# Two running totals as split single-pass matmuls, one slab part ordered behind a small one, and three products moved between VectorE and GpSimd

## The chip, the cores and the metric

The kernel runs on one core of one Trainium2 chip. The metric is the device time in microseconds (us) of one launch that computes two whole layers. Three runs of the kernel before gave 1693.34, 1693.60 and 1693.99 us; their median is 1693.6 us.

Engine names follow the profile: PE is the matmul engine (TensorE) and PEld its weight loads, DVE is VectorE, ACT is ScalarE, POOL is GpSimd, SP is the engine that issues the large loads.

## What is computed

A decoder trunk of two equal layers over 512 tokens of width 1024, all in float32. In each layer four token mixers share one input projection; the change touches three of them.

```python
def ssd_chunked(x, dt, a, bmat, cmat):            # Mamba-2 branch
    cs = jnp.cumsum(dtf * a.reshape(ng, r), axis=2)
    ...
def gla_chunked(q, k, v, log_a):                  # gated linear attention
    b = jnp.cumsum(log_a.reshape(bsz, nc, CHUNK, nh, dk), axis=2)
    b_last = b[:, :, -1]
    q_dec = qf * jnp.exp(b)
    k_inv = kf * jnp.exp(-b)
    k_end = kf * jnp.exp(b_last[:, :, None] - b)
    ...
def forgetting_attention(q, k, v, f_logit, q_gain, k_gain):
    qf = rms_norm(q, q_gain) * (dh ** -0.5)
    kf = rms_norm(k, k_gain)
    s = jnp.einsum('bhqd,bkhd->bhqk', q_blk, kf) + c_blk[..., :, None] - ck[..., None, :]
    ...
```

After the mixers come the gated merge, an output projection, and a feed-forward block of hidden width 2816.

## The kernel before, in words

**Weights.** All weights stream from HBM in slabs of 8 blocks of 128x128 (tile `wr`). `convert()` turns a slab into two parts: ACT casts a high part `wh` in the type float32r (`split`, line 208), and DVE subtracts it from the original to make a low part `wl` (line 209). `block()` hands out the blocks in order and asks for slabs two ahead of the one in use. Every projection is then three float32r matmuls for one block (`mm3`: high by high, high by low, low by high), 512 columns wide. `mm2` is the form with two matmuls, where one operand is exact in the high part alone and the other is a pair (high, low). A matmul whose operands are plain float32 goes through the same line 194, and the trace shows it as two records of TensorE.

**Order.** Each branch is a generator: `ssd()`, `gla()`, `ret()`, `fox()`, one after the other. `drain()` runs a branch, and at each `yield` it pulls some microseconds of filler from a list: projections of later branches, gate projections and up projections (`ups`, which ends in DVE line 1201). So the small matmuls of a branch stand between long runs of 512-column filler matmuls, and the chain of vector work between two yields has the filler as its cover. The framework plans the order of each engine's instructions ahead of the run, by its own timeline; each engine then runs its queue in that order. `order(a, b)` puts instruction `a` behind instruction `b` in the plan.

**The places of the change**, with the line numbers of the kernel before:

- In `ssd()`, line 707: the running total of `dta` (128 tokens by 32 columns) is one plain float32 matmul against `Uf`, a triangle of ones. `dts`, the split pair of the same `dta`, is already there for two other totals (`dflat`).
- In `gla()`, lines 863 to 866: `la` holds the logarithms of the gate in two tiles of 128x512; line 865 makes them on DVE. Line 873: four plain float32 matmuls for each `j` (0 and 1) form the running total in chunks of 64 with `ubd`, a block triangle of ones that float32r holds exactly. `la` is the stationary operand there. Lines 874 to 887 then form the decayed queries and keys; line 887 is the product for `k_end`, on POOL for both `j`. Line 915 transposes its results on PE.
- In `fox()`, line 1051 scales the query gain by 0.125, and line 1066 is the product of each of `q0`, `q1`, `k0`, `k1` (128x512) with its gain and its inverse norm, on DVE. `newton` (lines 373 to 375) refines the inverse norm just before. `stack()` (lines 1074 to 1084) splits the results for the scores.
- In `fox()`, `value()`: three calls for each head `hd`, with `runs` starting at (0, 0), (0, 2) and (2, 2). Each transposes probabilities, splits them (lines 208 and 209, widths 384, 512 and 384) and multiplies the values.

Of the kernel before, what the change touches and what calls it, by code (L numbers as in the profile page):

```python
# [10 lines left out]
F32 = mybir.dt.float32  # L11
# [3 lines left out]
ALU = mybir.AluOpType  # L15
# [3 lines left out]
P = 128  # L19
# [109 lines left out]
def trunk(ctx: ExitStack, tc: tile.TileContext, keys, qkeys, xin, pos, wst, wsq, par, ext, cst, out):  # L129
    nc = tc.nc  # L130
    V, A, G, T = nc.vector, nc.scalar, nc.gpsimd, nc.tensor
# [61 lines left out]
    def mm(o, l, r, start, stop):  # L193
        T.matmul(o, lhsT=l, rhs=r, start=start, stop=stop, skip_group_check=True)  # L194
# [7 lines left out]
    def mm2(o, l, r, start, stop):  # L202
        pairs = [(a, r) for a in l] if isinstance(l, tuple) else [(l, b) for b in r]
        for i, (a, b) in enumerate(pairs):
            mm(o, a, b, start and i == 0, stop and i == 1)

    def split(src, hi, lo):
        seen["copy"] = A.copy(out=hi, in_=src)  # L208
        V.tensor_tensor(out=lo, in0=src, in1=hi.bitcast(F32), op=ALU.subtract)  # L209
        return hi, lo  # L210

    def split_tile(t):
        return split(t, TT(F32R), TT(F32R))
# [4 lines left out]
    seen = {"set": None, "last": None}  # L218

    def order(a, b):  # L220
        tc.add_manual_dep(a.ins, b.ins.name, mybir.DependencyInfo(mybir.DependencyClass.NoSync, mybir.DependencyReason.DATA), reason="table")
# [31 lines left out]
    def convert():  # L253
        n = len(ready)
        if n < SLABS:
            far = n % (BLOCKS // SLAB) in TOKEN
            hi, lo = (piece("wh", 16), piece("wl", 48)) if far else (piece("wh"), piece("wl"))
            for h in halves(n):
                split(raw[n][:, h], hi[:, h], lo[:, h])
            ready.append((hi, lo))  # L260
            raw[n] = None

# [33 lines left out]
    o, w = PAR_OFF["ln1"]  # L296
# [47 lines left out]
    lst, bones, ubd, uo = (R(n) for n in ("lst", "bones", "ubd", "uo"))  # L344
    sel8 = R("sel8").rearrange("p (g r) -> p r g", g=2)
    sel4, selc = R("sel4"), R("selc")
    U, ones = uo[:, :P], uo[:, P:2 * P]
    Uf = U.bitcast(F32)
# [96 lines left out]
    def layer(l, n1, scope):  # L445
# [5 lines left out]
        def PR(n):  # L451
            o, w = PAR_OFF[n]
            return pr[:, l, o:o + w]
# [153 lines left out]
        dta = SM([P, NB, 8], "dta", 1)  # L607
# [6 lines left out]
        ps = MX()  # L614
# [62 lines left out]
        def ssd():  # L677
            Bt, Ct = xs[4], xs[5]
            pw = MX()
            dflat = tuple(t.rearrange("p c h -> p (c h)") for t in dts)  # L680
# [15 lines left out]
            for ps in pcb:  # L696
                t = TT()
# [3 lines left out]
            ps = MX()  # L701
# [2 lines left out]
            btok = TT()  # L704
            A.copy(out=btok, in_=ps)
            ps = MX()
            mm(ps[:32, :P], dta.rearrange("p c h -> p (c h)"), Uf, True, True)
            rows = stacked_rows(ps, 32, "blk8")
            heads = stacked_rows(ps, 32, "blkc", "blkc")
            ch, cl = (sp.tile([32, P], F32R, tag=n, name=nm(n), bufs=1) for n in ("csh", "csl"))  # L710
# [10 lines left out]
            for c in range(NB):  # L721
                ps = MX()
                for i in range(4):
                    T.transpose(ps[:, i * P:(i + 1) * P], xs[i][:, c * P:(c + 1) * P], ident)  # L724
                t = TT()
# [17 lines left out]
            for c in range(NB - 1):  # L743
                ps = parts[c]
                t = hp[c // 2][:, (c % 2) * 256:(c % 2 + 1) * 256]
# [8 lines left out]
            for r in range(4):  # L754
                ps = MX()
                mm(ps[:, P:], sel[:, r * P:(r + 1) * P], rows[:, P:], True, True)
                t = TT()
# [64 lines left out]
            for g in range(2):  # L822
                sq = []
                for ii in range(2):
                    t = TT()
# [6 lines left out]
            for g in range(2):  # L832
                ps = MX()
# [3 lines left out]
            for g in range(2):  # L837
                r = rstd_of(pn[g], 256)
                for ii in range(2):
                    i = 2 * g + ii  # L840
# [4 lines left out]
        gq, gk = [None] * 2, [None] * 2  # L845
# [3 lines left out]
        def gla():  # L849
            la, pl = [], []  # L850
            for half in range(2):
                ps = MX()
                pv = ps.rearrange("p (c n) -> p c n", c=2)
                for b in range(2):
                    tb = 2 * half + b
                    mm(pv[:, b], glrT[:, tb * P:(tb + 1) * P], w2, True, True)
                pl.append(ps)
                t = TT()
# [4 lines left out]
            for h_, t in enumerate(la):  # L863
                act(out=t, in_=t, func=AF.Ln, bias=one)
                V.scalar_tensor_tensor(out=t, in0=pl[h_], scalar=0.0, in1=t, op0=ALU.min, op1=ALU.subtract)
                la[h_] = t
            yield 2
            qd, ki, ke, dcs = [], [], [], []
            for j in range(2):
                ps = MX()  # L870
                for tb in range(NB):
                    o = (tb % 2) * 256 + j * P
                    mm(ps[:, tb * P:(tb + 1) * P], la[tb // 2][:, o:o + P], ubd.bitcast(F32), True, True)
                e = TT()
                act(out=e, in_=ps, func=AF.Exp, scale=1.0 / 16)
                V.tensor_tensor(out=gq[j], in0=gq[j], in1=e, op=ALU.mult)
                en = TT()
                act(out=en, in_=ps, func=AF.Exp, scale=-1.0 / 16)
                V.tensor_tensor(out=en, in0=gk[j], in1=en, op=ALU.mult)
                bl = SM([P, 8], "bl", 2)  # L880
                p8 = ps.rearrange("p (n t) -> p n t", n=8)
                V.tensor_copy(out=bl, in_=p8[:, :, 63])
                dc = SM([P, 8], "dc", 2)
                act(out=dc, in_=bl, func=AF.Exp, scale=1.0 / 16)
                V.tensor_tensor(out=e.rearrange("p (n t) -> p n t", n=8), in0=bl.unsqueeze(2).broadcast_to([P, 8, 64]), in1=p8, op=ALU.subtract)
                act(out=e, in_=e, func=AF.Exp, scale=1.0 / 16)
                G.tensor_tensor(out=e, in0=gk[j], in1=e, op=ALU.mult)  # L887
                qd.append(gq[j])
                ki.append(en)
                ke.append(e)  # L890
                dcs.append(dc)
# [11 lines left out]
            for half, ps in enumerate(pa):  # L903
                t = TT()
                (A.copy if half else V.tensor_copy)(out=t, in_=ps)
                for par_ in range(2):
                    u = t[64 * par_:64 * par_ + 64]
# [4 lines left out]
            for j in range(2):  # L912
                ps = MX()
                for tb in range(NB):
                    T.transpose(ps[:, tb * P:(tb + 1) * P], ke[j][:, tb * P:(tb + 1) * P], ident)  # L915
                t = TT()
# [4 lines left out]
            for tb in range(NB):  # L921
                for j in reversed(range(2)):
                    for par_ in range(2 if tb < NB - 1 else 1):
                        rs = slice(64 * par_, 64 * par_ + 64)
                        pv = pk[par_].rearrange("p (c j n) -> p c j n", c=NB, j=2)
                        for half in range(2):
                            hd = 2 * j + half
# [18 lines left out]
            for j in range(2):  # L946
                for tb in range(NB):
                    for par_ in range(2):
                        rs = slice(64 * par_, 64 * par_ + 64)
                        for half in range(2):  # L950
                            hd = 2 * j + half
# [93 lines left out]
        def fox():  # L1045
# [2 lines left out]
            fox_squares()  # L1048
            yield
            g8 = SM([P, 1], "g8", 1)  # L1050
            V.tensor_scalar(out=g8, in0=PR("fqn"), scalar1=0.125, scalar2=None, op0=ALU.mult)
            qk = fq + fk
            pn = []
            for q in fsq:
                ps = MX()
# [3 lines left out]
            for ps in pn:  # L1059
                u = TT()  # L1060
                act(out=u, in_=ps, func=AF.Ln, scale=1.0 / 64, bias=eps)
                rs_.append(u)
            for i, u in enumerate(rs_):
                act(out=u, in_=u, func=AF.Exp, scale=-0.5)
                newton(u, pn[i], 64)
                V.scalar_tensor_tensor(out=qk[i], in0=qk[i], scalar=g8 if i < 2 else PR("fkn"), in1=u, op0=ALU.mult, op1=ALU.mult)
            yield 2

            stk = {}
# [36 lines left out]
            def value(hd, runs, zs, po):  # L1106
                ps, W = MX(), 0
                at = []
                for kb, q0 in runs:
                    at.append(W)  # L1110
                    for qb in range(q0, 2 * (q0 // 2) + 2):
                        T.transpose(ps[:, W:W + P], zs[qb][:, kb * P:(kb + 1) * P], ident)  # L1112
                        W += P
                hi, lo = TT(F32R), TT(F32R)
                split(ps[:, :W], hi[:, :W], lo[:, :W])
                for (kb, q0), o in zip(runs, at):
                    q1 = 2 * (q0 // 2) + 2
                    n = (q1 - q0) * P
                    cols = slice(q0 * P, q1 * P)
                    v = fv[kb][:, hd].rearrange("p s d -> p (s d)")  # L1120
                    mm(po[:, cols], v, hi[:, o:o + n], kb == 0, False)
                    mm(po[:, cols], v, lo[:, o:o + n], False, kb >= 2 * (q0 // 2))
# [12 lines left out]
            t = None  # L1135
            step = 0
            for hd in range(NH):
                if hd % 2 == 0:
                    t = TT()
# [296 lines left out]
        a, u = FT([P, 2, S]), FT([P, 2, S])  # L1436
# [5 lines left out]
        hi, lo = split(a, FT([P, 2, S], F32R), FT([P, 2, S], F32R))  # L1442
# [130 lines left out]
```

## Time and profile before

| what | value |
|---|---|
| median of three runs | 1693.6 us |
| the profiled execution, own time | 1694.17 us |
| its span | 1692.5 us |
| PE busy in the span | 1684.7 us |
| DVE busy | 1199.7 us |
| ACT busy | 874.9 us |
| POOL busy | 198.0 us |
| granted TensorE clock | 1.0 |

A row of the timeline reads: start in us from the span's start, length in us, engine, line, operation, what it writes and reads, shape, count of merged instructions, and in brackets the idle time of the engine before it with what ended it. Matmuls overlap in the pipeline, so the length of a matmul row is longer than its share of PE's time: what a matmul costs is read from the distance between starts. A row of the waits reads: who waited for whom, total in us, times, longest.

### The profile page before, as it was taken

How to read it: one execution, taken by the hardware profiler on the slowest of the kernel's cores; microseconds unless marked ns; L12 is line 12 of the kernel's file. 1: busy time of each engine (PE TensorE's matmuls, PEld its weight loads, DVE VectorE, ACT ScalarE, POOL GpSimd, SP SyncE). 2: the span in 40 equal slices, each digit the busy share in tenths (PEclk: the TensorE clock that was granted, in tenths of full speed). 3: DMA queues.
4: the chain of work that ended last, by engine and by line, in shares of the span. 5: the costliest groups of instructions: out<-in, count | busy, mean ns of one | idle time of the engine just before them, and what ended most of it. 6: DMA issues, size and time to landing. Idle time of an engine off the chain costs nothing.

```text
span 1692.5 us, 25395 instructions
## 1 busy us (share of the span) xinstructions
PE 1684.7 (100%) x10286; PEld 1468.8 (87%) x10286; DVE 1199.7 (71%) x1690; ACT 874.9 (52%) x1206; POOL 198.0 (12%) x201
## 2 busy tenths in 40 slices
PE   9999999999999999999999999999999999999999
PEld 8888888888888999998988788888888889999998
DVE  6867676777677676676787776667776686767666
ACT  5436533555357556464544374346544484655643
POOL 3021100022101010101020211001221010101010
PEclk9999999999999999999999999999999999999999
DMA  6322222222235656575333222222222365665653
GB/s 207 111 77 75 88 75 76 88 87 88 77 100 165 180 136 186 128 195 117 90 104 110 85 65 86 88 78 85 88 87 77 105 189 153 151 174 139 185 107 106
DMA packets 54838, 194.95 MB, mean 115 GB/s; under 512 B 6208, under 2 KB 6848, under 8 KB 54720
## 3 DMA queue, kind: packets, MB, share of 16 engines
q1 hardware_dynamic: 45936, 161.87, 30.1%
q0 software_dynamic: 8640, 31.46, 10.5%
q8 instruction: 80, 1.31, 0.3%
q14 instruction: 38, 0.31, 0.1%
q10 hardware_dynamic: 144, 0.00, 0.0%
HBM read 191.21 MB, written 2.10 MB: 114 GB/s over the span
## 4 chain that ended last, share of the span: by engine, by line
PE 97%; DVE 1%; ACT 1%; POOL 0%; issue 0%; POOLq 0%; DVEq 0%
PE mm L194 65%; PE mx L194 31%; PE mx L1112 1%; DVE f L1456 0%; DVE x L1457 0%; ACT wh L208 0%; DVE wl L209 0%; PE mx L724 0%; POOL t L887 0%; DVE t L374 0%; ACT L227 0%; ACT g L232 0%; DVE t L1201 0%; PE mx L984 0%; PE mx L915 0%
## 5 line engine op out<-in xcount | busy, mean ns | idle before, releaser
L208 ACT CAST wh<-wr 128x1024 fp32r<-128x1024 f32 (+1 forms) x239 | 250.1, 1047 | 352.6 <-PE mm L194 200.3
L194 PE MATMUL mm<-xh,wh 128*128 128x512 f32 (+1 forms) x1184 | 428.5, 362 | 1.0 <-DVE t L1201 0.9
L194 PE MATMUL mm<-xl,wh 128*128 128x512 f32 (+1 forms) x1184 | 427.5, 361 | 0.0
L194 PE MATMUL mm<-xh,wl 128*128 128x512 f32 (+1 forms) x1184 | 427.4, 361 | 0.0
L209 DVE TENSOR_TENSOR wl<-wr,wh 128x1024 fp32r<-128x1024 f32 (+1 forms) x219 | 278.3, 1271 | 105.7 <-ACT wh L208 103.5
L194 PEld LDWEIGHTS mm<-xh,wh 128*128 128x128 f32 x1184 | 222.4, 188 | 36.0 <-DVE t L1201 1.7
L194 PEld LDWEIGHTS mm<-xh,wl 128*128 128x128 f32 x1184 | 222.4, 188 | 33.6
L194 PEld LDWEIGHTS mm<-xl,wh 128*128 128x128 f32 x1184 | 222.4, 188 | 33.6 <-issue 0.7
L194 PE MATMUL mm<-t,wh 128*128 128x512 f32 x448 | 139.6, 392 | 0.0
L194 PE MATMUL mx<-xl,wh 128*128 128x256 f32 (+1 forms) x448 | 137.9, 309 | 0.0
L194 PE MATMUL mx<-xh,wh 128*128 128x256 f32 (+1 forms) x448 | 135.9, 312 | 0.0
L1320 POOL DMA_DIRECT2D wl<-in_wsq_dram x60 | 51.9, 865 | 517.8 <-ACT wl L1319 352.3
L194 PE MATMUL mx<-f,wh 128*128 128x512 f32 x352 | 108.2, 390 | 0.0
L194 PE MATMUL mm<-f,wh 128*128 128x512 f32 (+1 forms) x360 | 106.4, 385 | 0.0
L194 PEld LDWEIGHTS mm<-t,wh 128*128 128x128 f32 x448 | 83.3, 188 | 17.2
L209 DVE TENSOR_TENSOR l<-rq,wh 128x1024 fp32r<-128x1024 f32 x60 | 73.3, 1221 | 32.8 <-ACT wh L208 18.6
L194 PE MATMUL mx<-xh,wl 128*128 128x256 f32 (+1 forms) x288 | 91.5, 327 | 0.0
L194 PEld LDWEIGHTS mx<-xh,wh 128*128 128x128 f32 x448 | 84.6, 189 | 5.1
L194 PEld LDWEIGHTS mx<-xl,wh 128*128 128x128 f32 x448 | 84.2, 188 | 5.3
L194 PE MATMUL mm<-t,wl 128*128 128x512 f32 x224 | 87.4, 390 | 0.0
L208 ACT CAST wh<-rq 128x1024 fp32r<-128x1024 f32 x60 | 63.0, 1050 | 43.8 <-PE mm L194 21.5
L194 PEld LDWEIGHTS mm<-f,wh 128*128 128x128 f32 x360 | 67.1, 188 | 13.3
(280 smaller groups left out, 3391.3 us busy)
## 6 DMA issues: line engine op xcount, KB each, us to landing
wr<-in_wst_dram SPq DMA_DIRECT2D x217, 512.0 KB, 3.5
rq<-in_wsq_dram SPq DMA_DIRECT2D x60, 512.0 KB, 5.5
wl<-in_wsq_dram POOLq DMA_DIRECT2D x60, 512.0 KB, 7.5
wr<-in_wsq_dram SPq DMA_DIRECT2D x20, 512.0 KB, 7.5
out_dram<-x SPq DMA_DIRECT2D x7, 256.0 KB, 2.0
x<-in_x_dram SPq DMA_DIRECT2D x3, 512.0 KB, 8.0
x<-in_x_dram SPq DMA_DIRECT2D x2, 256.0 KB, 4.4
wr<-in_wst_dram SPq DMA_DIRECT2D x2, 256.0 KB, 3.8
```

The source lines that it names most:

```text
L194: T.matmul(o, lhsT=l, rhs=r, start=start, stop=stop, skip_group_check=True)
L208: seen["copy"] = A.copy(out=hi, in_=src)
L209: V.tensor_tensor(out=lo, in0=src, in1=hi.bitcast(F32), op=ALU.subtract)
L1112: T.transpose(ps[:, W:W + P], zs[qb][:, kb * P:(kb + 1) * P], ident)
L1320: G.dma_start(out=lo, in_=wsq[j], accum_op=ALU.add)
```

## The change

Five edits:

- The total of `dta` in `ssd()` becomes `mm2` of the split pair `dflat` against the float32r triangle `U`: two float32r matmuls for one plain float32 one.
- The tiles `la` in `gla()` are split into high and low float32r parts (one ACT copy and one DVE subtraction for each of two tiles), and the eight totals become `mm2` of the pair against `ubd`.
- The product of line 887 runs on DVE for `j` = 1 and stays on POOL for `j` = 0.
- In `fox()` the gain of the keys is folded into that of the queries, so that the products for `k0` and `k1` are plain products of two tensors; they move from DVE to POOL.
- In `value()`, for the first head and the third call, the low part of the slab that was converted last is ordered behind the low part of this call's own split.

```diff
     def split(src, hi, lo):
         seen["copy"] = A.copy(out=hi, in_=src)
-        V.tensor_tensor(out=lo, in0=src, in1=hi.bitcast(F32), op=ALU.subtract)
+        seen["low"] = V.tensor_tensor(out=lo, in0=src, in1=hi.bitcast(F32), op=ALU.subtract)
         return hi, lo
...
                 split(raw[n][:, h], hi[:, h], lo[:, h])
+            seen["slab"] = seen["low"]
             ready.append((hi, lo))
...
-            mm(ps[:32, :P], dta.rearrange("p c h -> p (c h)"), Uf, True, True)
+            mm2(ps[:32, :P], dflat, U, True, True)
...
-                la[h_] = t
+                la[h_] = split_tile(t)
...
-                    mm(ps[:, tb * P:(tb + 1) * P], la[tb // 2][:, o:o + P], ubd.bitcast(F32), True, True)
+                    mm2(ps[:, tb * P:(tb + 1) * P], tuple(a[:, o:o + P] for a in la[tb // 2]), ubd, True, True)
...
-                G.tensor_tensor(out=e, in0=gk[j], in1=e, op=ALU.mult)
+                (V if j else G).tensor_tensor(out=e, in0=gk[j], in1=e, op=ALU.mult)
...
-            V.tensor_scalar(out=g8, in0=PR("fqn"), scalar1=0.125, scalar2=None, op0=ALU.mult)
+            V.scalar_tensor_tensor(out=g8, in0=PR("fqn"), scalar=0.125, in1=PR("fkn"), op0=ALU.mult, op1=ALU.mult)
...
-                V.scalar_tensor_tensor(out=qk[i], in0=qk[i], scalar=g8 if i < 2 else PR("fkn"), in1=u, op0=ALU.mult, op1=ALU.mult)
+                if i < 2:
+                    V.scalar_tensor_tensor(out=qk[i], in0=qk[i], scalar=g8, in1=u, op0=ALU.mult, op1=ALU.mult)
+                else:
+                    G.tensor_tensor(out=qk[i], in0=qk[i], in1=u, op=ALU.mult)
...
                 split(ps[:, :W], hi[:, :W], lo[:, :W])
+                if (hd, runs[0]) == (0, (2, 2)):
+                    order(seen["slab"], seen["low"])
```

## The prediction

> **What bounds the kernel now.** I read the page's busy times and the shares of the chain that ended last, then the waits of PE.
>
> ```profile
> PE 1684.7 (100%) x10286; PEld 1468.8 (87%) x10286; DVE 1199.7 (71%) x1690; ACT 874.9 (52%) x1206; POOL 198.0 (12%) x201
> PE 97%; DVE 1%; ACT 1%; POOL 0%; issue 0%; POOLq 0%; DVEq 0%
> PE mx L194 <- DVE t L209: 1.2, 2, 0.7
> PE mm L194 <- DVE t L1201: 0.9, 2, 0.4
> PE mx L915 <- POOL t L887: 0.6, 1, 0.6
> ```
>
> PE has work for the whole span, and the chain is PE for 97% of it. The waits that PE shows while the layers run add up to 2.7 us. So two things can change the time: the matmul time itself, and these few waits or new ones like them. Work taken off DVE, ACT or POOL counts only where PE waits for it. This caps the gain: an edit that touches a few microseconds of PE cannot move 1693.6 us far.
>
> **The total in gla().** First what PE spends on the eight float32 matmuls of one layer, then what float32r matmuls with full weights cost, then what the columns alone cost.
>
> ```profile
> 189.24 1.95 PE L194 MATMUL mx<-cr,t 128*128 128x128 f32 x16
> 190.94 0.48 PE L194 MATMUL mm<-xh,wh 128*128 128x512 f32 x1
> 191.25 0.40 PE L194 MATMUL mm<-xl,wh 128*128 128x512 f32 x1
> ...
> 93.86 0.51 PE L194 MATMUL mx<-dts,cr 128*128 128x32 f32 x4
> 94.30 1.16 PE L194 MATMUL mx<-t,t 64*128 64x128 f32 x16
> ...
> 447.29 19.80 PE mm L194 x87
> ```
>
> The last row is of the chain: 87 matmuls of 512 columns in 19.80 us, 0.228 us each, so 128 columns would be 0.057 us. The eight float32 matmuls stand as 16 records. From 189.24 to the start of the second filler matmul at 191.25 are 2.01 us; less one filler matmul of 0.228 us that leaves 1.78 us, or 0.111 us a record. The replacement is also 16 matmuls of 128 columns: two for each of eight. Their price is bounded by 0.057 us below (columns alone) and by the row at 93.86 above: four float32r matmuls of only 32 columns, each with its own 128-column weights, take 0.44 us until the next starts, 0.11 us each. With so few columns it can only be the change of weights that costs 0.11. In gla() `la` is the stationary operand, so every one of the 16 changes its weights. I take 0.11 us: 16 x 0.11 = 1.76, a saving of **0.0 us** a layer, with 16 x (0.111 - 0.057) = 0.86 us as the other end.
>
> [...]
>
> **The split that feeds it** adds, in each layer, two ACT copies and two DVE subtractions of 128x512 between line 865 and the total.
>
> ```profile
> 184.45 1.06 ACT L208 CAST wh<-wr 128x1024 fp32r<-128x1024 f32 x1
> 190.55 2.07 ACT L232 ACTIVATE t<-mx 128x512 f32<-128x512 f32 x4 [5.04 <-PE mx L194]
> ...
> 185.29 0.68 DVE L865 SCALAR_TENSOR_TENSOR t<-mx,t 128x512 f32<-128x512 f32 x1
> 185.88 1.21 DVE L209 TENSOR_TENSOR wl<-wr,wh 128x1024 fp32r<-128x1024 f32 x1
> 191.18 0.69 DVE L876 TENSOR_TENSOR t<-t,t 128x512 f32<-128x512 f32 x1 [4.08 <-ACT t L232]
> ```
>
> The second `la` is there at 185.97. Its copy is half a slab's cast (0.53 us, say 0.6), its subtraction is like line 876 (0.69 us). Behind the slab's low part, which ends at 187.09, the two subtractions end at 188.5; PE wants the total at 189.24. Both engines then sit idle for 4 to 5 us, so the rest of their queues has room. With the slab's cast ahead of the copy as well, and its low part behind that, I get 185.97 + 1.06 + 0.6 + 1.21 + 0.69 = 189.5: 0.3 us late a layer. I take 0, bounds 0 and +0.3 a layer. Filler matmuls cover it; without them PE would wait the full 1.3 us.
>
> **The total in ssd().**
>
> ```profile
> 96.35 0.40 PE L194 MATMUL mm<-xh,wh 128*128 128x512 f32 x1
> 96.68 0.41 PE L194 MATMUL mx<-cr,dta 128*32 128x128 f32 x2
> 97.02 0.50 PE L194 MATMUL mm<-xl,wh 128*128 128x512 f32 x1
> 97.35 0.39 PE L194 MATMUL mm<-xh,wl 128*128 128x512 f32 x1
> ...
> L194 PEld LDWEIGHTS mx<-cr,dta 128*32 128x32 f32 x4 | 0.3, 108 | 0.7 <-ACT t L705 0.7
> ```
>
> From 96.35 to 97.35 are 1.00 us; two filler matmuls are 0.46 of it, and the wait before 96.68 (0.33 less 0.23) another 0.10, which is for ACT line 705 and stays. So the two float32 records and the slow start behind them cost 0.44 us. The new form is two matmuls of 128 columns with 32-column weights, whose load is short (last row, and 0.7 us is idle). Nearest row: columns alone, 2 x 0.057 = 0.11 us; with full loads it would be 0.22. I take 0.11, a saving of **0.33 us** a layer (bounds 0.22 and 0.43), 0.66 in all. The pair is ready well before, since the totals at 93.86 read it.
>
> **The product on DVE for j = 1.** In the first layer the transposes of `j` = 0 pass without a wait, in the second those of `j` = 1 follow at once and wait.
>
> ```profile
> 198.12 0.66 PE L915 MATMUL mx<-cs,t 128*128 128x128 f32 x4
> 198.53 0.48 PE L194 MATMUL mm<-xh,wl 128*128 128x512 f32 x1
> ...
> 1030.90 0.66 PE L915 MATMUL mx<-cs,t 128*128 128x128 f32 x4
> 1032.13 0.66 PE L915 MATMUL mx<-cs,t 128*128 128x128 f32 x4 [0.57 <-POOL t L887]
> ...
> 1028.51 1.22 DVE L209 TENSOR_TENSOR wl<-wr,wh 128x1024 fp32r<-128x1024 f32 x1
> 1028.68 0.63 ACT L232 ACTIVATE t<-t 128x512 f32<-128x512 f32 x1
> 1028.79 3.29 POOL L887 TENSOR_TENSOR t<-t,t 128x512 f32<-128x512 f32 x2 [41.35 <-ACT dc L232]
> L887 POOL TENSOR_TENSOR t<-t,t x4: 1262/1388/2061, 195.8 to 1030.8; 128x512 f32<-128x512 f32 x4
> ```
>
> Four transposes need 0.41 us (198.12 to 198.53); in the second layer the next four start 1.23 us after the first, so PE loses 1.23 - 0.41 = 0.82 us to two POOL products in a row. After the change the factor for `j` = 1 is there at 1029.31 (ACT row), the slab's low part leaves DVE at 1029.73, and 0.69 us later, at 1030.4, the product is done, 0.9 us before PE wants it at 1031.31. The wait goes: **0.82 us**. What is late next is the product of `j` = 0 on POOL, done at 1028.79 + 2.06 = 1030.85, just where PE starts it now. In the first layer the edit is hidden. If DVE were 0.9 us later here the gain would begin to shrink, so its bounds are 0 and 0.82.
>
> **The key products in fox()** leave DVE for POOL.
>
> ```profile
> 325.28 0.68 DVE L375 SCALAR_TENSOR_TENSOR t<-t,t 128x512 f32<-128x512 f32 x1
> 327.02 0.75 DVE L1066 SCALAR_TENSOR_TENSOR t<-t,pr,t 128x512 f32<-128x512 f32 x1
> 327.80 0.62 ACT L1076 CAST t<-t 64x512 fp32r<-64x512 f32 x1 [2.44 <-DVE t L1066]
> 331.27 2.14 POOL L1205 TENSOR_TENSOR t<-t,t 128x512 f32<-128x512 f32 x1 [64.40 <-DVE t L1201]
> ```
>
> POOL is idle for 64 us before 331.27. The inverse norm of the last key is ready at 325.96. Even if POOL began `k0` only then, at 1.26 to 2.06 us it would be done between 327.2 and 328.0; DVE is done with it at 327.77 now, and ACT line 1076 takes it at 327.80. So that path is not later by more than 0.2 us, which the wait of 2.44 us there shows to be no wait of PE. DVE loses about 4 x 0.7 us in all. No PE wait hangs on these rows, so I take 0.
>
> **The order in value().**
>
> ```profile
> 366.83 0.48 DVE L1096 SCALAR_TENSOR_TENSOR t<-mx,cq,t 128x256 f32<-128x256 f32 x1
> 367.22 2.15 DVE L209 TENSOR_TENSOR wl<-wr,wh 128x1024 fp32r<-128x1024 f32 x1
> 369.30 0.55 DVE L209 TENSOR_TENSOR t<-mx,t 128x384 fp32r<-128x384 f32 x1
> ...
> 354.53 0.56 PE L194 MATMUL mx<-t,t 128*128 128x256 f32 x3 [0.53 <-DVE t L209]
> 354.99 0.74 DVE L1096 SCALAR_TENSOR_TENSOR t<-mx,cq,t 128x512 f32<-128x512 f32 x1
> ...
> 367.00 1.29 POOL L1205 TENSOR_TENSOR t<-t,t 128x512 f32<-128x512 f32 x1 [8.79 <-DVE t L1201]
> ```
>
> The third call of head 0 comes with the second score of head 1, 256 wide: it is the small part at 369.30, behind the slab's at 367.22. These two change places, and the slab's part ends 0.5 us later. But PE's wait for line 209 is at 354.53, before the fourth score of head 0 (512 wide): that is the first call, which the edit leaves alone. So I take 0; a slab is wanted two slabs later, which hides the 0.5 us.
>
> **Sum.** 0.66 + 0.82 = 1.48 us off. The profiled execution would go from 1694.17 to 1692.7 (span 1692.5 to 1691.0); its excess over the median of 1693.6 is 0.6 us, and against that median I forecast **1692.1 us**. A measurement of this kernel tells 0.2%, or 3.4 us, from no change, so this is "the same".
>
> **Rivals.**
>
> - *Columns set the price in gla().* 2 x 0.86 = 1.72 us more: 1690.4 us. For it: the name of the edit. Against it: the row at 93.86. Chance 0.05.
> - *The new plan also loses the old waits.* Every engine's order is planned anew, and the waits for lines 209 and 1201 (1.2 + 0.9 us) may fall away: 1692.1 - 2.1 = 1690.0 us. For it: they come from a large DVE instruction that stands just ahead of a small one. Against: no edit touches those places, and DVE was not short of time before 354.53. Chance 0.14.
> - *The new plan makes as many waits as there are now.* 2.1 us more: 1694.2 us. The new split, and the DVE product for `j` = 1, stand in DVE's queue ahead of parts that PE needs. Chance 0.13.
> - *POOL's key products hold up DVE* (ends slower). At 367.22 a slab's low part took 2.15 us in place of 1.22 while a POOL product of 1.29 us ran from 367.00. If each of the four key products stops DVE for its 1.29 us where PE waits for DVE next, as it does twice for line 1201 in this stretch, that is 5.2 us: 1692.1 + 5.2 = 1697.3 us; if DVE gets back its own 4 x 0.7 us, 1694.5. It decides once the backlog on DVE outlasts the free PSUM banks that PE still has. Against: DVE is 71% busy and gets idle time soon after. Chance 0.11, half of it at the high end.
> - *Nothing is gained* (the wait in the second layer stays, or moves to `j` = 0): 1692.9 us, within the forecast's own range.
>
> [...]
>
> **Chances.** Forecast case (1691.0 to 1693.4) 0.57, the rivals 0.05, 0.14, 0.13 and 0.11. Faster by over 0.2% (below 1690.2) needs the second rival and a little more, or both of the first two: 0.13. Slower by over 0.2% (above 1697.0) needs the high end of the fourth: 0.07. The same: 0.80. The range that leaves out 2 in 10 goes from 1689.7 to 1694.9 us: it takes in the first three rivals and the lower end of the fourth.
>
> **What would show it.** In the profile after: 16 records of the gla() total still 0.11 us apart, and their stretch of PE still near 1.8 us (at 0.06 apart the first rival holds); the two ssd() records some 0.06 us apart, with the next filler matmul at once behind them; no wait of line 915 for line 887 in the second layer; the two line 209 parts near 367 exchanged with no change of PE's waits; the key products on POOL, with newton or slab parts on DVE stretched beside them if the fourth rival acts. The forecast is wrong if PE's waits add up to more than about 4 us, or if a wait stands before the gla() total.

## The result and the profile after

| | before | after |
|---|---|---|
| median of 22 runs, us | 1693.51 (1693.01 to 1693.99) | 1695.59 (1694.92 to 1696.96) |
| ratio, 95% interval | | 1.0013 (1.0007 to 1.0019) |
| profiled execution, us | 1694.17 | 1695.55 |
| its span, us | 1692.5 | 1693.8 |

The kernel became 2.1 us slower where 1.5 us faster was forecast. That is within 0.2%, but 0.7 us above the forecast's range. First the page's busy times and the shares of its chain, then PE's waits (who waited for whom, total us, times, longest), all of the kernel after:

```profile
PE 1684.2 (99%) x10286; PEld 1468.4 (87%) x10286; DVE 1197.9 (71%) x1692; ACT 877.4 (52%) x1210; POOL 206.8 (12%) x203
PE 98%; DVE 1%; issue 0%; ACT 0%; POOL 0%; DVEq 0%; POOLq 0%
```

```profile
PE mm L194 <- DVE wl L209: 1.7, 2, 0.8
...
PE mx L194 <- DVE t L209: 0.9, 3, 0.3
PE mx L194 <- ACT t L208: 0.9, 2, 0.5
PE mm L194 <- DVE t L1207: 0.9, 2, 0.4
```

PE is the bound as before and its work is no longer: 1684.2 us busy against 1684.7. The wait for line 887 (0.6 us) is gone. Three kinds of wait make up for it: for a slab's low part (`wl`, twice, 1.7 us), for a small high part (ACT line 208, twice, 0.9 us) and for small low parts three times in place of two. With lines 1207 and 494 (0.9 and 0.3 us) they add up to 4.7 us, above the 4 us that the prediction named as a sign of being wrong.

**The steps that were to gain did gain at their places.** PE's timeline of the kernel after, at the totals of `ssd()` and `gla()`:

```profile
96.20 0.39 PE L194 MATMUL mm<-xh,wh 128*128 128x512 f32 x1
96.43 0.28 PE L194 MATMUL mx<-cr,dts 128*32 128x128 f32 x2
96.55 0.44 PE L194 MATMUL mm<-xl,wh 128*128 128x512 f32 x1
96.83 0.40 PE L194 MATMUL mm<-xh,wl 128*128 128x512 f32 x1
...
190.20 0.34 PE L194 MATMUL mx<-cr,t 128*128 128x128 f32 x2
190.37 0.45 PE L194 MATMUL mm<-xh,wh 128*128 128x512 f32 x1
190.66 0.40 PE L194 MATMUL mm<-xl,wh 128*128 128x512 f32 x1
...
191.81 1.68 PE L194 MATMUL mx<-cr,t 128*128 128x128 f32 x14
193.33 0.44 PE L194 MATMUL mm<-xh,wh 128*128 128x512 f32 x1
193.61 0.39 PE L194 MATMUL mm<-xl,wh 128*128 128x512 f32 x1
```

In `ssd()` two filler matmuls and the two records of the total now take 0.63 us (96.20 to 96.83), where they took 1.00 us. In `gla()` the sixteen records stand as 2 + 14: 0.17 us for the first two and 1.52 us for the rest, and the filler matmul behind each group is 0.06 and 0.05 us slower to be followed than the usual 0.23. That is 1.80 us, against 1.78 before. In the second layer the eight transposes of line 915 now follow one another without a wait (1033.53 to 1034.37).

**The loss stands in fox().** PE's timeline of the kernel after, where the third call of head 0 runs in the first layer:

```profile
360.11 0.39 PE L194 MATMUL mm<-xh,wh 128*128 128x512 f32 x1
360.34 0.40 PE L194 MATMUL mm<-xl,wh 128*128 128x512 f32 x1
360.57 0.71 PE L1116 MATMUL mx<-cs,t 128*128 128x128 f32 x5
361.73 0.39 PE L194 MATMUL mx<-t,t 128*128 128x256 f32 x1 [0.46 <-ACT t L208]
362.46 0.74 PE L194 MATMUL mx<-t,t 128*128 128x256 f32 x4 [0.34 <-DVE t L209]
...
364.37 0.29 PE L1116 MATMUL mx<-cs,t 128*128 128x128 f32 x1
365.51 0.50 PE L194 MATMUL mm<-xh,wl 128*128 128x512 f32 x1 [0.85 <-DVE wl L209]
```

A block is three filler matmuls: high by high, low by high, high by low. The first two of a block run at 360.11 and 360.34; the next matmul that needs this slab's low part comes only at 365.51, and waits for `wl`. So from 360.57 on PE has no filler but two matmuls at 363.27. The transposes and scores stand nearly bare, and their own waits, which filler covered before, show too. The three gaps lose about 2.3 us: 360.57 to 361.73 for five transposes, 361.73 to 362.46 for one score of 256 columns, 364.37 to 365.51 for one transpose; the usual distances are about 0.11 us for each of these. The second layer has the same three gaps from 1200.6 on.

Why `wl` is late stands in DVE's timeline, before and then after:

```profile
343.25 1.23 DVE L209 TENSOR_TENSOR wl<-wr,wh 128x1024 fp32r<-128x1024 f32 x1
...
349.72 1.23 DVE L209 TENSOR_TENSOR wl<-wr,wh 128x1024 fp32r<-128x1024 f32 x1 [0.36 <-ACT wh L208]
...
352.79 1.23 DVE L209 TENSOR_TENSOR wl<-wr,wh 128x1024 fp32r<-128x1024 f32 x1 [1.31 <-ACT wh L208]
353.93 0.55 DVE L209 TENSOR_TENSOR t<-mx,t 128x384 fp32r<-128x384 f32 x1
```

```profile
347.46 1.68 DVE L209 TENSOR_TENSOR wl<-wr,wh 128x1024 fp32r<-128x1024 f32 x1 [0.26 <-ACT wh L208]
...
353.40 0.56 DVE L209 TENSOR_TENSOR t<-mx,t 128x384 fp32r<-128x384 f32 x1 [2.13 <-PE mx L194]
...
361.71 0.69 DVE L209 TENSOR_TENSOR t<-mx,t 128x512 fp32r<-128x512 f32 x1 [1.89 <-ACT t L208]
...
363.31 0.55 DVE L209 TENSOR_TENSOR t<-mx,t 128x384 fp32r<-128x384 f32 x1
363.78 2.91 DVE L209 TENSOR_TENSOR wl<-wr,wh 128x1024 fp32r<-128x1024 f32 x2
```

The small part of the third call is now at 363.31, and behind it stand two slab parts. Before, slab parts stood at 349.72 and 352.79; after, nothing of a slab runs between 349.14 and 363.78, though DVE is idle for 2.13 and 1.89 us in that time. The first of the two is the slab that the edit names. `seen["slab"]` is the slab that the *program* had converted last when it reached this call; in the plan of before that conversion ran at 349.72, and the slab's first block starts on PE at 359.58. (An experiment below confirms which part it is: the third slab converted after the call is the one at 367.22, three parts behind 349.72.) The part of 352.79 was queued behind the held one.

To add up such gaps I took each pair of neighbouring matmuls in the trace: the distance of their starts, less the usual one for the first one's shape (0.227 us for 512 columns, 0.170 for 384, 0.114 for 256, 0.113 for fewer), where that leaves more than 0.06 us. In us, by stretch of the span, for the two kernels and for the experiments that the next section tells of:

| stretch | before | after | order alone | after without order | key products alone | the same, cast first | totals and product |
|---|---|---|---|---|---|---|---|
| start to 60 | 3.01 | 2.81 | 3.05 | 3.00 | 2.25 | 2.42 | 2.20 |
| 60 to 305: `ssd`, `gla`, layer 1 | 5.97 | 5.80 | 5.97 | 5.80 | 5.97 | 5.97 | 5.79 |
| 305 to 355.5: `fox`, first call | 1.88 | 1.61 | 1.60 | 2.87 | 3.08 | 1.88 | 1.90 |
| 355.5 to 447: rest of `fox` | 1.48 | 3.71 | 3.69 | 1.73 | 1.49 | 1.48 | 1.48 |
| 855 to 1145: layer 2, `ssd`, `gla` | 6.05 | 4.77 | 6.03 | 4.76 | 6.03 | 6.05 | 4.76 |
| 1145 to 1199: `fox`, first call | 2.02 | 0.98 | 1.61 | 1.90 | 1.90 | 1.90 | 2.10 |
| 1199 to 1290: rest of `fox` | 1.47 | 3.61 | 3.71 | 2.66 | 2.66 | 2.65 | 1.39 |
| all, with what is left out | 22.21 | 23.50 | 26.14 | 23.34 | 23.60 | 23.70 | 20.32 |
| span | 1692.5 | 1693.8 | 1696.3 | 1693.2 | 1693.3 | 1693.6 | 1690.4 |

From before to after: -0.17 and -1.28 in `ssd()` and `gla()`; +2.23 and +2.14 at the third call; -0.27 and -1.04 at the first call, whose small part no longer has a slab's part ahead of it. With the start and the end of the span it is +1.29, and the span grew by 1.3. The table counts only what is above the usual distance. By the starts of the same matmul in both traces the two stretches gain 0.04 and 1.32 us, together 1.36 of the forecast's 1.48: in the first layer, a longer wait for line 494 (by 0.15 us) and a shift of 0.2 us behind the total of `gla()` take back nearly all that `ssd()` gains. The start of the span differs by up to 0.9 us between these traces, so totals of single traces are good to about that.

### The profile page after: what moved, and what is told of

Read it like the earlier page. It is cut to its first block, busy times and chain, and to the rows that moved or that the text cites. A ratio compares the mean times of both kernels' runs of the same rounds, so it can differ in the third digit from the quotient of the medians.

```text
span 1693.8 us, 25399 instructions
## 1 busy us (share of the span) xinstructions
PE 1684.2 (99%) x10286; PEld 1468.4 (87%) x10286; DVE 1197.9 (71%) x1692; ACT 877.4 (52%) x1210; POOL 206.8 (12%) x203
## 4 chain that ended last, share of the span: by engine, by line
PE 98%; DVE 1%; issue 0%; ACT 0%; POOL 0%; DVEq 0%; POOLq 0%
PE mm L194 66%; PE mx L194 31%; PE mx L1116 0%; DVE f L1462 0%; DVE x L1463 0%; PE mx L725 0%; DVE wl L209 0%; DVE t L209 0%; DVE t L375 0%; DVE t L1207 0%; PE mx L916 0%; PE mx L985 0%; DVE t L374 0%; ACT t L208 0%; PE mx L704 0%
## 5 line engine op out<-in xcount | busy, mean ns | idle before, releaser
L209 DVE TENSOR_TENSOR wl<-wr,wh 128x1024 fp32r<-128x1024 f32 (+1 forms) x219 | 273.6, 1251 | 110.1 <-ACT wh L208 106.9
L209 DVE TENSOR_TENSOR l<-rq,wh 128x1024 fp32r<-128x1024 f32 x60 | 73.2, 1220 | 32.9 <-ACT wh L208 18.6
```

The source lines that it names most:

```text
L209: seen["low"] = V.tensor_tensor(out=lo, in0=src, in1=hi.bitcast(F32), op=ALU.subtract)
```

## The experiments

Twelve kernels ran, in three groups that each share the runs of the kernel before. The medians are in us; one difference has an interval of about +-1.5 us, so differences under that rest on the traces, not on the time.

### The order edit alone

```diff
-        V.tensor_tensor(out=lo, in0=src, in1=hi.bitcast(F32), op=ALU.subtract)
+        seen["low"] = V.tensor_tensor(out=lo, in0=src, in1=hi.bitcast(F32), op=ALU.subtract)
...
+            seen["slab"] = seen["low"]
...
+                if (hd, runs[0]) == (0, (2, 2)):
+                    order(seen["slab"], seen["low"])
```

> The kernel before with the order edit alone. Theory A (the order edit holds back a slab that PE needs): 2.5 to 3.5 us above the kernel before, and in the last branch of both layers new PE waits for line 209 and line 208, about 2.2 us in each layer, while the wait of the first call of value() shrinks. Theory B (the key products on POOL hold up DVE): no difference within 0.7 us, and no new waits. Theory C (no edit alone does it, the new plan of all five together does): under 1.5 us above.

Measured: 1697.15 against 1693.58, ratio 1.0022 (1.0013 to 1.0031). PE's timeline shows the same three gaps, and DVE's the same pair of slab parts, behind the small part of the third call:

```profile
363.60 0.55 DVE L209 TENSOR_TENSOR t<-mx,t 128x384 fp32r<-128x384 f32 x1
364.06 2.91 DVE L209 TENSOR_TENSOR wl<-wr,wh 128x1024 fp32r<-128x1024 f32 x2
```

Nothing else is edited here, so the order edit makes these waits by itself: 2.2 us in each layer in the table, 0.7 us of it given back at the two first calls. That is 3.8 us of span and 3.6 us of time.

### The change without the order edit

```diff
-                if (hd, runs[0]) == (0, (2, 2)):
-                    order(seen["slab"], seen["low"])
```

> The kernel after without the order edit. Theory A: 1 to 2 us below the kernel before, about 1692, and the waits for line 209 in the last branch as in the kernel before. Theory B: still 1.5 us or more above the kernel before. Theory C: anything between, with other waits than in either kernel.

Measured: 1695.13 against 1693.58, ratio 1.0009 (1.0000 to 1.0018). The three gaps of the third call are gone, and yet the kernel is still slower than before. PE's timeline shows a new place, the first call:

```profile
352.93 0.91 PE L194 MATMUL mx<-t,t 128*128 128x256 f32 x5
355.67 0.56 PE L194 MATMUL mx<-t,t 128*128 128x256 f32 x3 [1.82 <-DVE t L209]
```

Five scores need 0.75 us (1192.49 to 1193.24 in the trace after, where nothing waits), so PE loses 1.98 us here, where it lost 0.69 before. So one more edit costs time, and the order edit hides it: the slab's part that stands ahead of this small part here is one of the two that it holds.

### The two totals alone

```diff
-            mm(ps[:32, :P], dta.rearrange("p c h -> p (c h)"), Uf, True, True)
+            mm2(ps[:32, :P], dflat, U, True, True)
...
-                la[h_] = t
+                la[h_] = split_tile(t)
...
-                    mm(ps[:, tb * P:(tb + 1) * P], la[tb // 2][:, o:o + P], ubd.bitcast(F32), True, True)
+                    mm2(ps[:, tb * P:(tb + 1) * P], tuple(a[:, o:o + P] for a in la[tb // 2]), ubd, True, True)
```

> The kernel before with the two running totals as split single passes alone. By the forecast's terms: 0.7 us below the kernel before, all of it from ssd(); the wait of line 915 for line 887 in the second layer stays. If the matmuls of the gla() total cost their columns alone: 1.7 us more, 2.4 us below. If the new plan makes waits: above the kernel before.

Measured: 1692.18 against 1693.58, ratio 0.9992 (0.9983 to 1.0000). This is the fastest kernel of the study, 1.4 us below before and 3.4 below after. About 0.6 of it belongs to `ssd()` (shown below). For the rest the trace has a plain reason: in the second layer the wait of line 915 is gone, though the product is still on POOL for both `j`. The new plan puts filler between the two groups of transposes.

### The key products alone

```diff
-            V.tensor_scalar(out=g8, in0=PR("fqn"), scalar1=0.125, scalar2=None, op0=ALU.mult)
+            V.scalar_tensor_tensor(out=g8, in0=PR("fqn"), scalar=0.125, in1=PR("fkn"), op0=ALU.mult, op1=ALU.mult)
...
-                V.scalar_tensor_tensor(out=qk[i], in0=qk[i], scalar=g8 if i < 2 else PR("fkn"), in1=u, op0=ALU.mult, op1=ALU.mult)
+                if i < 2:
+                    V.scalar_tensor_tensor(out=qk[i], in0=qk[i], scalar=g8, in1=u, op0=ALU.mult, op1=ALU.mult)
+                else:
+                    G.tensor_tensor(out=qk[i], in0=qk[i], in1=u, op=ALU.mult)
```

> The kernel before with the key products on POOL and the gain folded into the queries alone. Theory A: no difference within 0.5 us. Theory B: 1.5 to 3 us above the kernel before, with PE waits for DVE in the stretch after the products.

Measured: 1696.64 against 1693.58, ratio 1.0019 (1.0010 to 1.0028). PE loses 1.89 us at the first call. The chain behind it can be read over three engines. First ACT's timeline before, then ACT's, SP's and DVE's of this kernel (SP's row: first load in the stretch from 338 us on, length up to the end of the last, count), and SP's of before at the end:

```profile
341.29 1.05 ACT L208 CAST wh<-wr 128x1024 fp32r<-128x1024 f32 x1
...
344.93 1.92 ACT L232 ACTIVATE g<-g 128x2048 f32<-128x2048 f32 x1
```

```profile
342.49 1.92 ACT L232 ACTIVATE g<-g 128x2048 f32<-128x2048 f32 x1
...
345.72 1.05 ACT L208 CAST wh<-wr 128x1024 fp32r<-128x1024 f32 x1
...
352.00 1.05 ACT L208 CAST wh<-wr 128x1024 fp32r<-128x1024 f32 x1 [1.09 <-DMA wr<-in_wst_dram]
```

```profile
348.50 21.52 SPq L246 DMA_DIRECT2D wr<-in_wst_dram  x5
```

```profile
346.80 2.90 DVE L209 TENSOR_TENSOR wl<-wr,wh 128x1024 fp32r<-128x1024 f32 x2 [0.26 <-ACT wh L208]
...
353.08 1.22 DVE L209 TENSOR_TENSOR wl<-wr,wh 128x1024 fp32r<-128x1024 f32 x1 [1.51 <-ACT wh L208]
354.23 0.55 DVE L209 TENSOR_TENSOR t<-mx,t 128x384 fp32r<-128x384 f32 x1
```

```profile
344.50 25.23 SPq L246 DMA_DIRECT2D wr<-in_wst_dram  x5
```

Before, ACT casts a slab at 341.29, ahead of the sigmoid of 2048 columns and its two table loads (1.28 us each). In the new plan the same cast stands behind them, at 345.72. The slab's low part (the first of the two at 346.80) ends at 348.48, 4.0 us later than before. It reads `wr`, of which there are two buffers, so the next load can start only behind it: at 348.50, where before it started at 344.50, directly after the low part of 343.25 to 344.48. The loaded slab's cast waits for the load until 352.00, its low part until 353.08, and the small part of the first call is queued behind that.

### The order edit on the slab that the prediction meant

```diff
             for h in halves(n):
                 split(raw[n][:, h], hi[:, h], lo[:, h])
+            if seen.get("hold"):
+                seen["hold"][1] -= 1
+                if seen["hold"][1] == 0:
+                    order(seen["low"], seen.pop("hold")[0])
...
                 split(ps[:, :W], hi[:, :W], lo[:, :W])
+                if (hd, runs[0]) == (0, (2, 2)):
+                    seen["hold"] = [seen["low"], 3]
```

It is made on the kernel before and holds the third slab converted after the call, in the program's order.

> The kernel before with the exchange that the forecast read into the order edit: the low part of the third call of value() of head 0 ahead of the slab part that stands just before it in the plan (the one at 367.22). Theory A1 (the edit costs because it takes hold of an earlier slab, which PE needs): no difference within 0.5 us. Theory A2 (any slab part put behind a small one there costs): 1 us or more above the kernel before.

Measured: 1693.56 against 1693.32, ratio 1.0002 (0.9993 to 1.0011). DVE's timeline shows the exchange:

```profile
367.95 0.56 DVE L209 TENSOR_TENSOR t<-mx,t 128x384 fp32r<-128x384 f32 x1 [1.01 <-POOL t L1211]
368.43 1.22 DVE L209 TENSOR_TENSOR wl<-wr,wh 128x1024 fp32r<-128x1024 f32 x1
```

The prediction's price, nothing, is right for the exchange that it described. The edit makes another one.

### The totals and the product of line 887

```diff
-                G.tensor_tensor(out=e, in0=gk[j], in1=e, op=ALU.mult)
+                (V if j else G).tensor_tensor(out=e, in0=gk[j], in1=e, op=ALU.mult)
```

It comes on top of the two totals.

> The two totals and the product of line 887 for j = 1 on DVE, without the key products on POOL and without the order edit. If the parts that gained add up: 1.4 us (the totals, as measured) and 0.8 to 0.9 us (the wait of line 915), so 2.2 us below the kernel before, about 1691.3 us. If a new plan eats it: about 1692.2 us, as with the totals alone.

Measured: 1692.24 against 1693.32, ratio 0.9992 (0.9984 to 1.0001). That is no more than the totals alone gave. Both ways of removing the second layer's wait earn the same microsecond; it can be earned once.

### The first call's small part ahead of a slab

This was meant as a kernel better than both. On top of the one above, the same holding code, with the first call in place of the third:

```diff
+                if (hd, runs[0]) == (0, (0, 0)):
+                    seen["hold"] = [seen["low"], 3]
```

> The same with the low part of the first call of value() of head 0 put ahead of the slab's low part that stands before it in the plan (the wait of 0.7 and 0.8 us for line 209). If that wait is the whole cost there: 1.5 us below the kernel without it, about 1689.8. If the filler behind it waits for its PSUM bank (line 1201) as well, half of that: 1690.5. If the held slab is missed later, as in the order edit: above it.

Measured: 1699.39 (six runs) against 1693.32, ratio 1.0031 (1.0019 to 1.0043). The kernel became slower by 6.1 us. PE's wait for the small part shrinks to 0.24 us, but two slab parts now stand behind it on DVE and ahead of line 1207, which empties a PSUM bank. PE's timeline and its table by stretch (length, busy us of PE, PEld, DVE, ACT and POOL with counts, granted clock, DMA share, GB/s):

```profile
354.15 0.30 PE L1116 MATMUL mx<-cs,t 128*128 128x128 f32 x1
356.62 0.74 PE L194 MATMUL mm<-t,wh 128*128 128x512 f32 x2 [2.17 <-DVE t L1207]
...
359.21 0.63 PE L194 MATMUL mm<-xh,wh 128*128 128x512 f32 x1
359.64 0.63 PE L194 MATMUL mm<-xl,wh 128*128 128x512 f32 x1
```

```profile
357.00:361.00 4.00, 4.00 (x13) 3.24 (x12) 3.28 (x9) 1.10 (x4) 2.68 (x4) 0.57 0.58 221
361.00:365.00 4.00, 4.00 (x20) 3.23 (x19) 2.01 (x4) 1.15 (x3) 0.00 (x0) 1.00 0.00 0
```

A wait of 2.36 us (2.47 from start to start, less 0.11 for the transpose) is followed by filler matmuls 0.43 us apart in place of 0.23: the clock granted is 0.57 on the mean of 357 to 361 us. So this wait is paid for twice, and it stands in both layers (the second one from 1196.48 on).

### The key products, with the first call's small part ahead

The holding code for the first call, as above, on top of the key products alone.

> The key products on POOL, with the low part of the first call of value() of head 0 ahead of the slab parts that stand before it. Theory P (the key products cost because the new plan makes that small part late; 1.9 us of wait in the first layer): 1.2 us or more below the kernel with the key products alone, so 1695.4 us or less. Theory L (POOL's products hold up DVE's own instructions beside them): within 0.5 us of 1696.6 us.

Measured: 1696.93 against 1693.32, ratio 1.0023 (1.0014 to 1.0031). The wait for the small part falls from 1.89 to 0.40 us, but the same 2.36 us wait for the bank comes in its place. The time is the one that theory L named, but the loss only moved, so this run doesn't tell whether the plan or a slowing of DVE beside POOL is its cause.

### The key products, with the slab's cast put back

On top of the key products alone; the sigmoid and its table load go behind the cast of that slab.

```diff
+            if n % (BLOCKS // SLAB) == 56:
+                for i in seen["sig"]:
+                    order(i, seen["copy"])
...
-                        act(out=st["t"], in_=st["t"], func=AF.Sigmoid)
+                        seen["sig"] = (act(out=st["t"], in_=st["t"], func=AF.Sigmoid), seen["pre"])
```

> The key products on POOL, and in the last branch one slab's cast put back ahead of the gate activation on ACT, where the kernel before has it. Theory D (the new plan puts that cast behind the activation, so the slab's low part and with it the next load of raw weights come some 4 us later, the small part of the first call waits behind that load, and where the wait nears 2 us the matmul clock drops as well): the first-layer wait of 1.9 us goes back to 0.7 us, the load is issued near 344, and the time falls from 1696.6 to 1695.2 us or less. Theory L (POOL's products hold up DVE's instructions beside them): within 0.5 us of 1696.6 us.

Measured: 1694.68 against 1693.24, ratio 1.0007 (0.9998 to 1.0016). About half of the 3.1 us is gone. SP's row for the same stretch as above:

```profile
343.72 25.41 SPq L246 DMA_DIRECT2D wr<-in_wst_dram  x5
```

The load starts 4.8 us earlier, and the first layer's `fox()` is back to the 1.88 and 1.48 us of before. The key products are still on POOL, so they didn't make that wait by slowing DVE; the moved cast did, through the late load. What is left stands mostly in the second layer, 1.1 us in the table, in waits for lines 1193 and 209 that this edit doesn't touch. The first of them (0.8 us, at 1195) only takes the place of the wait that the first call had before. The second (at 1220) is new. DVE's timeline of this kernel there:

```profile
1215.28 0.68 DVE L1134 TENSOR_TENSOR t<-mx,t 64x512 f32<-64x512 f32 x1 [2.06 <-ACT t L1133]
...
1219.03 1.22 DVE L209 TENSOR_TENSOR wl<-wr,wh 128x1024 fp32r<-128x1024 f32 x1
1220.16 0.55 DVE L209 TENSOR_TENSOR t<-mx,t 128x384 fp32r<-128x384 f32 x1
```

The small part that PE waits for stands behind a slab's part; before, it stood ahead of it (1217.82, then 1219.67). The last key product had ended at 1168.50, and DVE had caught up since: it was idle for 2.06 us before 1215.28. So the new plan makes this wait too, and not a hold of the key products on DVE.

### The gain folded, the products on DVE

```diff
-                    G.tensor_tensor(out=qk[i], in0=qk[i], in1=u, op=ALU.mult)
+                    V.tensor_tensor(out=qk[i], in0=qk[i], in1=u, op=ALU.mult)
```

Against the key products alone.

> The gain folded into the queries and the key products as plain products, but on DVE as before. Theories D and L both: no difference within 0.5 us of the kernel before, since its plan is that of the kernel before but for a few places. If the fold itself costs: 1 us or more above.

Measured: 1693.11 against 1693.24, ratio 1.0000 (0.9991 to 1.0009). Folding the gain shows no cost. What costs is the change of engine, with the plan that follows from it.

### One total, and one product, each alone

Only line 707 as `mm2`:

> The total of ssd() as a split single pass alone. By the forecast's term: 0.66 us below the kernel before (0.4 to 0.9). If the gain of the two totals together came from gla(): 0.2 us or less.

Measured: 1692.65 against 1693.24, ratio 0.9997 (0.9988 to 1.0006). Only the product of line 887 on DVE for `j` = 1:

> The product of line 887 for j = 1 on DVE alone. By the forecast's term: 0.82 us below the kernel before, and no wait of line 915 in the second layer. If the wait only moves to the product of j = 0: 0.2 us or less.

Measured: 1692.42 against 1693.24, ratio 0.9994 (0.9985 to 1.0002); PE's list of waits has none for line 887. The two differences, 0.59 and 0.82 us, are near the terms of the sum (0.66 and 0.82), but both intervals contain no change. The trace bears out the first: each `ssd()` stretch is 0.38 us shorter. The second agreement is partly luck: in the trace the second layer gains about 0.6 us there, the first layer gains 1.0 us between 203 and 254 us where the plan groups small matmuls otherwise, and two waits for casts of slabs near 1397 us take 0.9 us back.

## Why the prediction was wrong, point by point

- **The total in gla(): right.** The records stand 0.11 us apart in the new form too, and their stretch costs 1.80 against 1.78 us. The rival by columns alone falls: 14 records of 128 columns took 1.52 us to the next start, where columns alone would be 0.80 (14 x 0.057).
- **The split that feeds it: right.** No PE wait stands before either group of the total.
- **The total in ssd(): right.** 0.37 us a layer in the trace where 0.33 was forecast. That it is so near is partly luck: 0.10 of it is the wait for line 705, which I had left standing, and the new form costs 0.17 us where 0.11 was taken.
- **The product for j = 1: right, but not additive.** The wait goes, in the kernel after and with the edit alone. It is gone with the totals alone as well, which the prediction didn't see: a plan that puts filler between the two groups makes the edit needless.
- **The order in value(): this step failed.** The prediction read "the slab converted last" as the one that stands next to the small part on DVE (367.22 and 369.30), and priced that exchange, rightly, at nothing. The edit names a slab by the program's order, and that slab's part ran at 349.72, almost 20 us ahead of the small part. Held back to 363.78, it takes PE's filler away. The cover that I named, "a slab is wanted two slabs later", does not hold for it: its first block is due at 359.58 in the trace before, so the part now comes too late. The order edit alone costs 3.6 us.
- **The key products: this step failed too, though it doesn't show in the sum.** The prediction followed the path of a key, found it no later by more than 0.2 us, and took 0 because no wait of PE hangs on these rows. The bound on the path held. POOL's row and ACT's row that reads its result, in the kernel after:

```profile
324.01 1.65 POOL L1070 TENSOR_TENSOR t<-t,t 128x512 f32<-128x512 f32 x1 [57.46 <-DVE t L376]
...
325.69 0.62 ACT L1080 CAST t<-t 64x512 fp32r<-64x512 f32 x1 [0.53 <-POOL t L1070]
```

The first key is done at 325.66, 2.1 us earlier than on DVE before (327.77), and ACT takes it at once. What failed is the step from there to a cost of 0: it looked at the readers of the products, and not at what a new plan does with the other instructions in the same queues. The plan put a slab's cast on ACT behind the sigmoid, and two raw buffers carried the delay into a load and on to PE (1.2 us in the first layer, and a mean clock of 0.999 in 4 of 11 runs); in the second layer it put a slab's part ahead of a small part that PE waits for (1.1 us). Together the key products alone cost 3.1 us, of which putting the cast back returned about half. The slowing that the fourth rival names shows as well: in the kernel after, beside the first key product one of DVE's two query products took 1.79 us in place of 0.75. But no wait of PE of over 0.25 us follows from there up to the first call at 353 us, and at the first call the late load is the cause. That the measured 1695.6 us lies between the two ends of that rival (1694.5 and 1697.3) is luck.
- **Why the two losses are one in the sum.** Totals and product give -1.1 us, the order edit +3.6, the key products +3.1: that would be +5.6, and +2.1 was measured. The order edit takes away just the slab part that the key products make late, ahead of the first call; with both, the first call waits less than before (1.61 and 0.98 us in the table). -1.1 + 3.6 = +2.5 without the key products is near the measured +2.1, within the uncertainty of such sums; taking the order edit out alone gives back only 0.5 us, since the other loss then appears.
- **The rivals.** "As many waits as there are now" adds 2.1 us to the forecast (1694.2 us), of the 3.5 us by which the time lies above the forecast; it put the new waits in the split and the product, where there are none. The waits for line 209 at the first call did shrink, as the second rival had it; those for line 1201 (now 1207) stayed at 0.9 us.
- **The chances.** A net of nothing over 0.2% was right; the range was too narrow above, because two edits that change a planned order were priced at exactly nothing.

## What to carry to other kernels

An order edge binds the instruction that the program named, wherever the plan runs it: look up where that one stands now, and ask what it feeds and which buffer it holds, since with two raw buffers a late reader is a late load (here by 4.0 us). PE had no slack here (99% busy), and filler covered its small waits: the edit that delayed the filler's operands uncovered about 2.3 us of them in a layer. Nor did the prices of edits that change the plan add up (+5.6 us by the sum, +2.1 measured): measure each alone and all but each, and expect the same microsecond to be gained, or lost, only once.

## What the hardware showed that was not expected

Behind one wait of PE, of 2.36 us, the granted clock was lower. In the trace of the kernel with the first call's small part ahead (on top of the totals and the product) it is 0.50 in place of 1.00 from about 357.3 to 360.7, 3.4 us, worked out from the mean clock of two short stretches (0.81 in 357.2 to 357.4, 0.66 in 360.6 to 360.8); with matmuls 0.43 us apart in place of 0.23, about half speed, that is an estimated 1.7 us lost on top of the wait. All 6 runs of that kernel, and 5 of the 11 of the other with this wait (the key products with the first call's small part ahead), have a mean clock of 0.999 or 0.998 in place of 1.000. The first of these two kernels has the wait in both layers: four of its runs took 1699.27 to 1700.04 us (0.998, one of them 0.999) and two 1697.67 and 1697.75 us (0.999), about one such loss apart. With a longest wait of 1.9 to 2.0 us (the key products alone, and the change without the order edit) the mean clock is 0.999 in 4 of 11 runs each, and their median is 1.3 and 1.1 us above that of the others; for these there is no trace of the slow stretch itself. No run of the kernels with shorter waits, both of the main kernels among them, has it. Why the same wait has the lower clock behind it in some runs and not in others stays open.
